# A ninth Strassen step in five gate units, E added by transfers, and last products by halves

## The chip, the cores and the metric

The kernel runs on one core of a Trainium2 chip. The metric is the device time of one execution in microseconds. Before the change three runs took 2383.65 to 2385.43 us, median 2385.24.

## The reference

One hybrid decoder block on 256 tokens with 4096 channels, all float32:

```
h    = rmsnorm(x, norm_w)
proj = h @ w_in                       # 4096 -> 20480: u_p z_p u_c b_c c_c z_c (2048 each), g_logit (8192)
y_pool = pool(u_p) @ pool_w * pool_scale * silu(z_p)      # causal means over 2, 4, 8, 16 tokens
y_conv = b_c * (conv_b + conv3(c_c * u_c)) * silu(z_c)
br     = [y_pool, y_conv] @ w_branch                      # two times 2048 -> 4096
merged = sum over n of sigmoid(g_logit[n] + gate_b[n]) * br[n]
x      = x + merged @ w_out                               # 4096 -> 4096
return rmsnorm(x, final_norm_w)
```

Nearly all of the work is in three matrix products, with w_in, w_branch and w_out.

## The kernel before, in words

**Units.** The work is cut into 32 units, each of which makes 1024 output columns for all 256 tokens (two halves of 128 tokens on the partitions) in the tile R. In order: the convolution's cu0 cc0 cz0 cb0 cu1 cc1 cz1 cb1, the pooling's pz0 pu0 pz1 pu1, the eight gate units g0_0 g1_0 g0_1 g1_1 g0_2 g1_2 g0_3 g1_3 (branch, then column block), eight branch units b0_0 to b1_3, and four output units o0 to o3. A unit with 4096 rows of weights has 16 steps of 256 rows. Each step loads 1 MB of weights into one of three raw buffers by SP's queue.

**P and S steps.** Float32 accuracy comes from splitting each operand into a high part, rounded to the fast matmul format (an ACT copy), and a low part (a DVE subtraction), and from three products, high by high, high by low, low by high. A plain step (P) multiplies 2 row blocks x 2 token halves x 2 column halves, 8 products of three matmuls of 128x512 each: 24 matmuls. A Strassen step (S) treats the same as a 2x2 block product with 7 products: 21 matmuls. It needs sums of weights and so more of DVE: an addition into V, two additions in raw, and subtractions 1536, 1024 and 1024 wide; a P step needs two subtractions 1024 wide. In the program's order on DVE an S step is: addition into V, addition in raw, the 1536-wide subtraction (from ACT's 1536-wide copy), addition in raw, subtraction from V, subtraction from raw.

**The ring.** The split weights lie in a ring of 60 blocks (256 columns each); an S step takes 28, a P step 16. `pump` hands out work for a step up to three steps ahead of PE, as far as the ring has room, and raw buffers are loaded again once their step is split. Every engine works through its own instructions in the written order (`keep_in_program_order`).

**x and its sums.** The split x stays in the arena: pairs of row blocks with sums for Strassen (S operands) and without (P operands). The arena has sums for 7 pairs. An eighth pair, `LATE` (number 8), has its sums made early by `late_sums`, put away in DRAM (`late_d`), and fetched and split again in g0_0 (`late_split`) into a pool that takes the place of the tile Y; from then on the gate units can have 8 S steps. In which steps a unit has S is set by `spread_sequence` or `at_places`: before, g0_1 to g0_3 had P S P S P S P S S P S P S P S P. Steps of a unit are numbered from 0.

**Ends of units, and ticks.** The banks `sums` (E banks) are emptied by ACT to the tile E with the factor rin; the four banks `shared`, which hold the other Strassen products, are joined into R by an ACT copy and four DVE additions and subtractions (`joins`). When the last step of a unit is P, the shared banks are closed a step earlier, and the joins are put on `queue` then ("early"). `queue` holds small pieces of work; one is taken after every 6 matmuls (a tick), and `gap(n)` leaves n ticks free. `combine` then adds E to R: for most gate units by two DVE additions, for g0_0 and o0 by a transfer that accumulates (`move_add`, POOL's queue), which needs no DVE. The gate's bias gate_b is always added by such a transfer. After that the unit's epilogue is queued: one free tick, the sigmoid of R on ACT, and a store of R to `gates_d` by POOL. All this runs beside the next unit's matmuls.

**The end.** The last three steps of o3 are done token half by token half. `finish_half` adds a bank to R and squares it on ACT with a sum over the columns; `finish` makes 1/rms from these sums, scales the four column blocks (three of them fetched back from DRAM) and stores them.

Of the kernel before, what the change touches and what calls it, by code (L numbers as in the profile page):

```python
# [32 lines left out]
P = 128  # L33
# [23 lines left out]
def hybrid_block(ctx: ExitStack, tc: tile.TileContext, x, x_t, norm_t, w_first, w_in, pool_w, pool_scale,  # L57
# [68 lines left out]

    y_d = dram.tile([2, 2, P, 4, 2, T], F32, name="y_d")
    m_d = dram.tile([4, P, 4, 2, T], F32, name="m_d")
    late_d = dram.tile([P, 5, P], F32, name="late_d")
    z_d = dram.tile([2, P, 2, NU], F32, name="z_d")  # L130
    o_d = dram.tile([3, P, 2, NU], F32, name="o_d")

# [9 lines left out]
    def replace_by(name, place=upper):  # L142
        close(upper)
        close(place)
        place["stack"] = stack = ExitStack()
        ctx.enter_context(stack)
        return stack.enter_context(tc.tile_pool(name=name, bufs=1))

    Y = replace_by("y", lower).tile([P, 2, NU], F32, name="Y")

# [319 lines left out]
    def combine(u):  # L470

        d = u.dst
        if u.s:
            early = u.flags.get("joined")
            if not early:
                join(u)
            if u.name.startswith(('cu1', 'cz', 'pz')):

                queue.append(lambda: move_add(d, E))
                queue.extend(gap(9))  # L480
            elif u.name in ['g0_0', 'o0']:
# [48 lines left out]
    def gap(n):  # L530
        return [None] * n
# [567 lines left out]

    LATE = NP_X - 1  # L1100

    def late_sums():
        o = x_ops[LATE]
        h, l = (o.view[:, part].bitcast(F32) for part in range(2))
        q = sa[:, 4:8].rearrange("p (k t) c -> p k t c", t=2)
        add(q, h, l)
        q = q.rearrange("p k t c -> p k (t c)")
        mul(q, q, rbc[:, None].to_broadcast([P, 2, T]))
        sums_s(sa, [sa[:, i] for i in range(4, 8)])
        mul(sa[:, Q3], sa[:, Q3], std)  # L1110
        move(late_d[:, 0:4], sa[:, 0:4])
        move(late_d[:, 4], sa[:, A11])
# [211 lines left out]
    for u in units:  # L1324
        if u.name == "pu1":
            make_bands(1)
        if u is last_x:
            Y = replace_by("y_b", lower).tile([P, 2, NU], F32, name="Y")
            stages.append(replace_by("more").tile([P, 4, P], F32, name="sb"))

            in_y = [Y.rearrange("p a n -> p (a n)")[:, i * 4 * P:(i + 1) * 4 * P].rearrange("p (k c) -> p k c", k=4) for i in range(2)]
            stages.extend(in_y)
        if u is last:
            break
        for st in u.steps:
            assert st.prepared, (u.name, st.kind)
            run_step(u, st)
            state["now"] += 1
            if u is last_x and st is u.steps[12]:
                units_done[0] = True  # L1340
            if u.s and not u.flags.get("joined") and st is not u.steps[-1] and u.closed(*SHARED):
                assert not queue, u.name
                queue.extend(joins(u))
            pump()
            if u is units[units.index(last_x) - 1] and st is u.steps[14]:
                queue_fills()
            if u.name == "g0_0" and st is u.steps[2]:
                move(sa[:, 0:5], late_d)
# [57 lines left out]
    for c in range(3):  # L1406
        unpark(c)

    pre, pre_h, var_h, dev = (sb(name, [P, 2]) for name in ("pre", "pre_h", "var_h", "dev"))

    def ts(dst, a, s1, s2, op0, op1=ALU.bypass):
        pin(nc.vector.tensor_scalar(out=dst, in0=a, scalar1=s1, scalar2=s2, op0=op0, op1=op1))

    def finish_half(t, n):

        w = NH // (1 + n)
        for i in range(1 + n):
            cs = slice(n * NH + i * w, n * NH + (i + 1) * w)
            add(R[:, t, cs], bank_of(("E", t, n))[:, i * w:(i + 1) * w], R[:, t, cs])
            act(V[:, n, i * w:(i + 1) * w], R[:, t, cs], AF.Square, accum_out=ossq[:, t, 3 + n + i:4 + n + i])  # L1420
        if n == 0:
            mul(E[:, t, 0:NH], R[:, t, 0:NH], Y[:, 0, 0:NH])

    def finish(t):
        q, h, r, s, v = (a[:, t:t + 1] for a in (pre, pre_h, rout, dev, var_h))
        part = ossq[:, t, 5:6]
# [10 lines left out]
        for c, queue_ in ((0, nc.sync), (1, nc.scalar), (2, nc.sync), (3, nc.sync)):  # L1437
            if c == 1:
                act(parked[c][:, t], parked[c][:, t], scale=r)
            elif c == 0:  # L1440

                for n in range(2):
                    v = parked[c][:, t, n * NH:(n + 1) * NH]
                    pin(nc.vector.tensor_scalar(out=v, in0=v, scalar1=r, scalar2=None, op0=ALU.mult))
                    pin(queue_.dma_start(of[t * P:(t + 1) * P, n * NH:(n + 1) * NH], v))
                continue
            elif c == 2:
                pin(nc.vector.tensor_scalar(out=parked[c][:, t], in0=parked[c][:, t], scalar1=r, scalar2=None, op0=ALU.mult))
            else:
                pin(nc.vector.tensor_scalar(out=E[:, t, 0:NH], in0=E[:, t, 0:NH], scalar1=r, scalar2=None, op0=ALU.mult))  # L1450
                stt(E[:, t, NH:NU], R[:, t, NH:NU], r, Y[:, 0, NH:NU], ALU.mult, ALU.mult)
            pin(queue_.dma_start(of[t * P:(t + 1) * P, c * NU:(c + 1) * NU], E[:, t] if c == 3 else parked[c][:, t]))

    for t in range(2):
        for ns in ((0, 1),) if t == 0 else ((0,), (1,)):
            for st in tail:
                st.toks, st.halves, st.final = (t,), ns, (t, ns[-1]) == (1, 1)
                while not st.op.ready:
                    pop_fill(True)
                for g in st.groups():  # L1460
                    multiply(last, st, g)
            for n in ns:
                finish_half(t, n)
        finish(t)


# [47 lines left out]
```

## Time and profile before

| what | value |
|---|---|
| median of three runs | 2385.24 us |
| the profiled execution | 2384.67 us, its span 2383.0 us |
| PE | 2370.5 us busy, 99% of the span, 10558 matmuls |
| DVE | 2136.1 us busy, 90% |
| ACT | 1380.5 us busy, 58% |
| POOL | 78.3 us busy, 3% |
| TensorE clock granted | 0.998 |
| DMA | 550.92 MB, mean 231 GB/s |

PE is the engine of the matmuls, DVE the vector engine, ACT the scalar engine, POOL and SP issue transfers. The busy time of PE is modelled: matmuls are pipelined and overlap, so the distance from one matmul's start to the next says more than the 390 ns that the profile gives to each. In a timeline row stand the start, the time taken, engine, line, operation, result and sources, shapes, how many were merged (x3), and in brackets how long the engine was idle before and for whom. Rows are merged when equal operations follow each other. In a row of the windows view stand the window, its length, and for each engine the busy time and the number of instructions, then the granted clock, the DMA share and GB/s. L72 is the helper of all DVE additions, subtractions and products, L69 that of ACT, L1244 that of the matmuls, L94 that of the accumulating transfers, L91 that of the others from POOL.

### The profile page before, as it was taken

How to read it: one execution, taken by the hardware profiler on the slowest of the kernel's cores; microseconds unless marked ns; L12 is line 12 of the kernel's file. 1: busy time of each engine (PE TensorE's matmuls, PEld its weight loads, DVE VectorE, ACT ScalarE, POOL GpSimd, SP SyncE). 2: the span in 40 equal slices, each digit the busy share in tenths (PEclk: the TensorE clock that was granted, in tenths of full speed). 3: DMA queues.
4: the chain of work that ended last, by engine and by line, in shares of the span. 5: the costliest groups of instructions: out<-in, count | busy, mean ns of one | idle time of the engine just before them, and what ended most of it. 6: DMA issues, size and time to landing. Idle time of an engine off the chain costs nothing.

```text
span 2383.0 us, 27859 instructions
## 1 busy us (share of the span) xinstructions
PE 2370.5 (99%) x10558; PEld 1961.5 (82%) x10558; DVE 2136.1 (90%) x2162; ACT 1380.5 (58%) x1443; POOL 78.3 (3%) x148
## 2 busy tenths in 40 slices
PE   9999999999999999999999999999999999999998
PEld 7888888888888888888888888888888888888886
DVE  8899989889989978979999999999898898798998
ACT  7555655556555556556565655566664556565564
POOL 0010000000000000000000000000100001000000
PEclk9999999999999999999999999999999999999999
DMA  8455665655666655755776677667766667567667
GB/s 336 170 207 195 233 243 199 225 202 211 230 228 214 233 192 212 242 191 201 256 248 219 232 236 238 226 239 259 264 250 229 227 251 285 210 215 253 244 241 262
DMA packets 83158, 550.92 MB, mean 231 GB/s; under 512 B 9536, under 2 KB 9536, under 8 KB 21584
## 3 DMA queue, kind: packets, MB, share of 16 engines
q1 hardware_dynamic: 68800, 484.51, 54.4%
q0 software_dynamic: 13792, 63.58, 9.6%
q8 instruction: 82, 1.34, 0.2%
q10 hardware_dynamic: 432, 1.07, 0.1%
q14 instruction: 52, 0.43, 0.1%
HBM read 516.28 MB, written 25.49 MB: 227 GB/s over the span
## 4 chain that ended last, share of the span: by engine, by line
PE 94%; issue 3%; DVE 1%; DMA 1%; ACT 0%; DVEq 0%; ACTq 0%; POOLq 0%
PE sums L1244 73%; PE shared L1244 19%; PE shared L746 1%; PE shared L509 1%; DVE ring L72 1%; DMA R<-in_x_dram 1%; DMA raw<-in_w_out_dram 0%; DMA R<-E 0%; ACT ring L69 0%; DVE V L72 0%; PE shared L1008 0%; DVE raw L72 0%; DVE R L72 0%; PE shared L725 0%; PE shared L726 0%
## 5 line engine op out<-in xcount | busy, mean ns | idle before, releaser
L1244 PE MATMUL sums<-ring,arena 128*128 128x512 f32 x8031 | 1888.2, 390 | 0.0
L1244 PEld LDWEIGHTS sums<-ring,arena 128*128 128x128 f32 x8031 | 1504.9, 188 | 313.2 <-ACT E L69 0.6
L69 ACT ACTIVATE ring<-raw 128x1024 fp32r<-128x1024 f32 (+2 forms) x902 | 994.9, 1142 | 729.9 <-DVE raw L72 290.0
L72 DVE TENSOR_TENSOR ring<-raw,ring 128x1024 fp32r<-128x1024 f32 (+2 forms) x902 | 1171.9, 1329 | 167.5 <-ACT ring L69 129.9
L1244 PE MATMUL shared<-ring,arena 128*128 128x512 f32 x2079 | 526.0, 389 | 0.5 <-DVE ring L72 0.5
L1244 PEld LDWEIGHTS shared<-ring,arena 128*128 128x128 f32 x2079 | 390.0, 188 | 82.1 <-DVE ring L72 1.3
L69 ACT ACTIVATE ring<-V 128x1024 fp32r<-128x1024 f32 x180 | 190.2, 1056 | 124.8 <-DVE V L72 91.1
L72 DVE TENSOR_TENSOR V<-raw 128x1024 f32<-128x1024 f32 x180 | 219.2, 1218 | 4.9 <-DMA raw<-in_w_in_dram 3.1
L72 DVE TENSOR_TENSOR ring<-V,ring 128x1024 fp32r<-128x1024 f32 x180 | 219.2, 1218 | 2.5 <-ACT ring L69 2.5
L72 DVE TENSOR_TENSOR raw<-raw 128x512 f32<-128x512 f32 x180 | 124.5, 692 | 6.2
L72 DVE TENSOR_TENSOR raw<-V,raw 128x512 f32<-128x512 f32 x180 | 124.3, 691 | 5.4
L72 DVE TENSOR_TENSOR R<-R,E 128x1024 f32<-128x1024 f32 (+1 forms) x49 | 77.6, 1590 | 1.6 <-ACT E L69 0.9
L72 DVE TENSOR_TENSOR R<-R,shared 128x512 f32<-128x512 f32 x87 | 59.5, 683 | 13.3 <-ACT R L69 9.5
L69 ACT ACTIVATE E<-sums,rin 128x512 f32<-128x512 f32 x76 | 50.7, 687 | 26.7 <-PE sums L1244 26.7
L69 ACT ACTIVATE arena<-sa 128x512 fp32r<-128x512 f32 (+2 forms) x42 | 22.4, 560 | 36.0 <-DVE sa L72 35.3
L72 DVE TENSOR_TENSOR arena<-sa,arena 128x512 fp32r<-128x512 f32 (+2 forms) x42 | 24.4, 604 | 1.4 <-ACT arena L69 1.4
L69 ACT ACTIVATE E<-sums 128x512 f32<-128x512 f32 x40 | 22.3, 593 | 4.8 <-PE sums L1244 4.4
L509 PEld LDWEIGHTS shared<-ident,R 128*128 128x128 f32 x160 | 19.4, 140 | 4.2
L509 PE MATMUL shared<-ident,R 128*128 128x128 f32 x160 | 22.6, 272 | 0.0
L746 PE MATMUL shared<-ring 128*128 128x512 f32 x96 | 22.1, 389 | 0.0
L69 ACT ACTIVATE R<-R 128x2048 f32<-128x2048 f32 x8 | 15.4, 1920 | 11.4 <-DVE R L72 7.6
L72 DVE TENSOR_TENSOR R<-R,Y 128x1024 f32<-128x1024 f32 (+1 forms) x16 | 21.5, 1355 | 0.3
(142 smaller groups left out, 467.8 us busy)
## 6 DMA issues: line engine op xcount, KB each, us to landing
raw<-in_w_in_dram SPq DMA_DIRECT2D x318, 1024.0 KB, 4.9
raw<-in_w_branch_dram SPq DMA_DIRECT2D x64, 1024.0 KB, 5.5
raw<-in_w_out_dram SPq DMA_DIRECT2D x64, 1024.0 KB, 5.0
R<-in_gate_b_dram POOLq DMA_DIRECT2D x8, 1024.0 KB, 11.7
gates_d<-R POOLq DMA_DIRECT2D x8, 1024.0 KB, 9.1
R<-E POOLq DMA_DIRECT2D x6, 1024.0 KB, 8.6
raw<-in_pool_w_dram SPq DMA_DIRECT2D x4, 1024.0 KB, 4.7
Y<-gates_d POOLq DMA_DIRECT2D x4, 1024.0 KB, 7.4
```

The lines of the kernel that those rows point to most:

```text
L69: return pin(nc.scalar.activation(dst, src, func, **kw))
L72: return pin(nc.vector.tensor_tensor(out=dst, in0=a, in1=b, op=op))
L509: pin(nc.tensor.transpose(shared(j)[:, i * T + t * P:i * T + (t + 1) * P], src[:, t, c:c + P], ident))
L746: pin(nc.tensor.matmul(o, a[:, k, ts], b[:, k], start=(k, i) == (0, 0), stop=(k, i) == (3, 2)))
L1244: pin(nc.tensor.matmul(ps, lhs, rhs, start=n == 0, stop=n == u.total[b] - 1))
```

## The change

Five gate units, g0_1, g1_1, g0_2, g1_2 and g0_3, get nine S steps of 16, in the order P P S S P S S P S S P S S P S P. For the ninth, pair 7's sums are made by a second call of `late_sums`, ahead of step 42 (cz0's step 10), and stored in a second DRAM tile; they are fetched and split in g1_0 (`second_split`), three blocks in the pool that stands in Y's place and two in a pool above it. The matrices for the pooling's windows (`make_bands`) are therefore made ahead of step 118 (cb1's step 6) instead of step 33, since they take the place of tiles that `late_sums` needs. `combine` adds E by the accumulating transfer for g1_0, g0_1, g1_1, g0_2 and g1_2 as well; where the joins were early, the transfer of gate_b is issued first, then that of E, and 12 ticks are left free instead of 17. At the end, the last step's products of the last bank are done 256 columns at a time, the second half in another bank, the mean for the square root gets a tile of its own and is made first, and the first output block is stored in 256 and 768 columns instead of 512 and 512.

```diff
-    late_d = dram.tile([P, 5, P], F32, name="late_d")
+    late_d = [dram.tile([P, 5, P], F32, name=f"late_d{i}") for i in range(2)]
...
-            elif u.name in ['g0_0', 'o0']:
+            elif u.name in ['o0', 'g0_0', 'g1_0', 'g0_1', 'g1_1', 'g0_2', 'g1_2']:
 
                 queue.append(lambda: move_add(d, E))
                 if not early:
                     queue.append(lambda: move_add(d, u.added))
-                queue.extend(gap(17))
+                queue.extend(gap(12 if early else 17))
...
         if (n, c) in ((0,1),(1,1),(0,2),(1,2),(0,3),(1,0),):
             seq = spread_sequence(NS_X + 1, 1 if c else 2)
+        if (n, c) in ((0,1),(1,1),(0,2),(1,2),(0,3),):
+            seq = at_places({2,3,5,6,8,9,11,12,14})
...
-    def late_sums():
-        o = x_ops[LATE]
+    def late_sums(i):
+        o = x_ops[LATE - i]
...
+    def second_place():
+        o = x_ops[LATE - 1]
+        o.more, tiles = {}, []
+        for pool, blocks in ((lower["pool"], (Q3, Q5, Q6)), (replace_by("late_too"), (Q7, A11))):
+            q = pool.tile([P, 2, len(blocks), P], F32R, name="more_sums")
+            tiles.append(q)
+            for i, b in enumerate(blocks):
+                o.more[b] = q[:, :, i]
+        return tiles
+
+    def second_split():
+
+        o, src, q = x_ops[LATE - 1], (sa[:, 0:3], sa[:, 3:5]), []
+
+        def high():
+            q.extend(second_place())
+            for a, b in zip(q, src):
+                act(a[:, 0], b)
+
+        def low():
+            for a, b in zip(q, src):
+                sub(a[:, 1], b, a[:, 0].bitcast(F32))
+            o.more_ready = True
+        return [high, low]
...
-    before(23, late_sums)
-    before(33, make_bands, 0)
+    before(23, late_sums, 0)
+    before(42, late_sums, 1)
+    before(118, make_bands, 0)
...
+            if u.name == "g1_0" and st is u.steps[4]:
+                move(sa[:, 0:5], late_d[1])
+            if u.name == "g1_0" and st is u.steps[7]:
+                queue.extend(second_split())
...
     def finish(t):
...
         pin(nc.vector.tensor_reduce(out=q, in_=ossq[:, t:t + 1, 0:5], axis=mybir.AxisListType.X, op=ALU.add))
+        ts(m, q, 1.0 / D, EPS, ALU.mult, ALU.add)
         ts(h, q, -0.5 / D, -0.5 * EPS, ALU.mult, ALU.add)
-        ts(q, q, 1.0 / D, EPS, ALU.mult, ALU.add)
-        act(s, part, AF.Sqrt, scale=1.0 / D, bias=q)
+        act(s, part, AF.Sqrt, scale=1.0 / D, bias=m)
...
-                for n in range(2):
-                    v = parked[c][:, t, n * NH:(n + 1) * NH]
+                for a, b in ((0, NH // 2), (NH // 2, NU)):
+                    v = parked[c][:, t, a:b]
...
+                if (t, ns) == (1, (1,)) and st is tail[-1]:
+
+                    (b, mm, _), = st.groups()
+                    for i in range(2):
+                        cs = slice(i * NH // 2, (i + 1) * NH // 2)
+                        for k, (lhs, rhs) in enumerate(mm):
+                            pin(nc.tensor.matmul(shared(0)[:, 0:NH // 2] if i else bank_of(b)[:, cs], lhs, rhs[:, cs],
+                                                 start=i == 1 and k == 0, stop=k == len(mm) - 1))
+                        if i == 0:
+                            add(R[:, t, NH:NU], bank_of(b), R[:, t, NH:NU])
+                        else:
+                            add(R[:, t, NH + NH // 2:NU], shared(0)[:, 0:NH // 2], R[:, t, NH + NH // 2:NU])
+                        finish_part(t, 1, i, False)
+                    continue
```

More of the change, by code (lines that the diff above doesn't have):

```diff
@@ L146, in replace_by @@
         ctx.enter_context(stack)
-        return stack.enter_context(tc.tile_pool(name=name, bufs=1))
+        place["pool"] = stack.enter_context(tc.tile_pool(name=name, bufs=1))
+        return place["pool"]
     Y = replace_by("y", lower).tile([P, 2, NU], F32, name="Y")
@@ L1110, in late_sums @@
         mul(sa[:, Q3], sa[:, Q3], std)
-        move(late_d[:, 0:4], sa[:, 0:4])
-        move(late_d[:, 4], sa[:, A11])
+        move(late_d[i][:, 0:4], sa[:, 0:4])
+        move(late_d[i][:, 4], sa[:, A11])
     def late_place(pool, o, blocks):
@@ L1347, in hybrid_block @@
             if u.name == "g0_0" and st is u.steps[2]:
-                move(sa[:, 0:5], late_d)
+                move(sa[:, 0:5], late_d[0])
             if u.name == "g0_0" and st is u.steps[8]:
@@ L1407, in hybrid_block @@
         unpark(c)
-    pre, pre_h, var_h, dev = (sb(name, [P, 2]) for name in ("pre", "pre_h", "var_h", "dev"))
+    pre, pre_h, var_h, dev, mean = (sb(name, [P, 2]) for name in ("pre", "pre_h", "var_h", "dev", "mean_out"))
     def ts(dst, a, s1, s2, op0, op1=ALU.bypass):
@@ L1414, in finish_half, with finish_part @@
     def finish_half(t, n):
-        w = NH // (1 + n)
         for i in range(1 + n):
-            cs = slice(n * NH + i * w, n * NH + (i + 1) * w)
-            add(R[:, t, cs], bank_of(("E", t, n))[:, i * w:(i + 1) * w], R[:, t, cs])
-            act(V[:, n, i * w:(i + 1) * w], R[:, t, cs], AF.Square, accum_out=ossq[:, t, 3 + n + i:4 + n + i])
+            finish_part(t, n, i)
         if n == 0:
             mul(E[:, t, 0:NH], R[:, t, 0:NH], Y[:, 0, 0:NH])
+    def finish_part(t, n, i, sums=True):
+        w = NH // (1 + n)
+        if True:
+            cs = slice(n * NH + i * w, n * NH + (i + 1) * w)
+            if sums:
+                add(R[:, t, cs], bank_of(("E", t, n))[:, i * w:(i + 1) * w], R[:, t, cs])
+            act(V[:, n, i * w:(i + 1) * w], R[:, t, cs], AF.Square, accum_out=ossq[:, t, 3 + n + i:4 + n + i])
     def finish(t):
         q, h, r, s, v = (a[:, t:t + 1] for a in (pre, pre_h, rout, dev, var_h))
+        m = mean[:, t:t + 1]
         part = ossq[:, t, 5:6]
         pin(nc.vector.tensor_reduce(out=q, in_=ossq[:, t:t + 1, 0:5], axis=mybir.AxisListType.X, op=ALU.add))
+        ts(m, q, 1.0 / D, EPS, ALU.mult, ALU.add)
         ts(h, q, -0.5 / D, -0.5 * EPS, ALU.mult, ALU.add)
-        ts(q, q, 1.0 / D, EPS, ALU.mult, ALU.add)
-        act(s, part, AF.Sqrt, scale=1.0 / D, bias=q)
+        act(s, part, AF.Sqrt, scale=1.0 / D, bias=m)
         ts(v, part, -0.5 / D, h, ALU.mult, ALU.add)
@@ L1440, in finish @@
             elif c == 0:
-                for n in range(2):
-                    v = parked[c][:, t, n * NH:(n + 1) * NH]
+                for a, b in ((0, NH // 2), (NH // 2, NU)):
+                    v = parked[c][:, t, a:b]
                     pin(nc.vector.tensor_scalar(out=v, in0=v, scalar1=r, scalar2=None, op0=ALU.mult))
-                    pin(queue_.dma_start(of[t * P:(t + 1) * P, n * NH:(n + 1) * NH], v))
+                    pin(queue_.dma_start(of[t * P:(t + 1) * P, a:b], v))
                 continue
@@ L1462, in hybrid_block @@
             for n in ns:
-                finish_half(t, n)
+                if (t, n) != (1, 1):
+                    finish_half(t, n)
         finish(t)
```

## The prediction

> **What bounds the kernel now.** I read the page first (the chain that ended last), then PE's waits, then the five units that change, by windows.
>
> ```profile
> PE 94%; issue 3%; DVE 1%; DMA 1%; ACT 0%; DVEq 0%; ACTq 0%; POOLq 0%
> ```
> ```profile
> PE shared L1244 <- DVE ring L72: 0.5, 2, 0.3
> ```
> ```profile
> 1205.89:1614.63 408.74, 408.74 (x1801) 337.92 (x1801) 380.06 (x353) 243.93 (x234) 9.41 (x11) 1.00 0.67 232
> 1287.67:1369.42 81.75, 81.75 (x362) 67.59 (x361) 75.76 (x71) 48.51 (x48) 1.76 (x2) 1.00 0.68 232
> ```
>
> The chain is PE, and PE waits for DVE only twice, 0.5 us in all. The third fence is gate units g0_1 to g0_3 together, then g1_1 alone; its columns are length, then busy time of PE, PEld, DVE, ACT, POOL, then clock. The clock is full; PE needs all of a unit's 81.75 us and DVE 75.76 of them. DVE is the only engine near PE, so the question is whether it still keeps up with more Strassen steps. The pace of both is in these rows of g1_1 (PE, then DVE):
>
> ```profile
> 1313.65 0.84 PE L1244 MATMUL shared<-ring,arena 128*128 128x512 f32 x3
> ...
> 1323.85 0.84 PE L1244 MATMUL shared<-ring,arena 128*128 128x512 f32 x3
> ```
> ```profile
> 1313.76 1.22 DVE L72 TENSOR_TENSOR V<-raw 128x1024 f32<-128x1024 f32 x1
> 1315.01 0.69 DVE L72 TENSOR_TENSOR raw<-V,raw 128x512 f32<-128x512 f32 x1
> 1315.62 1.75 DVE L72 TENSOR_TENSOR ring<-raw,ring 128x1536 fp32r<-128x1536 f32 x1
> 1317.41 0.69 DVE L72 TENSOR_TENSOR raw<-raw 128x512 f32<-128x512 f32 x1
> ...
> 1319.29 1.23 DVE L72 TENSOR_TENSOR ring<-raw,ring 128x1024 fp32r<-128x1024 f32 x1
> 1320.43 1.22 DVE L72 TENSOR_TENSOR V<-raw 128x1024 f32<-128x1024 f32 x1
> ...
> 1329.39 1.22 DVE L72 TENSOR_TENSOR V<-raw 128x1024 f32<-128x1024 f32 x1
> ...
> 1371.61 0.68 DVE L72 TENSOR_TENSOR R<-R,shared 128x512 f32<-128x512 f32 x1
> 1372.21 1.22 DVE L72 TENSOR_TENSOR ring<-raw,ring 128x1024 fp32r<-128x1024 f32 x1
> ```
>
> PE starts an S and a P step (45 matmuls) 10.20 us apart: 0.2267 a matmul, S 4.76, P 5.44. On DVE an S step takes 1320.43 - 1313.76 = 6.67, and S with P 1329.39 - 1320.43 = 8.96, so P 2.29; a 1024-wide operation takes 1.14 (1320.43 - 1319.29), one of a join 0.60 (1372.21 - 1371.61). DVE thus loses 1.91 on PE in an S step behind an S, and gains 3.15 in a P step.
>
> **The change: PE's saving.** Five P steps become S: 15 matmuls x 0.2267 = 3.40 us. A unit has 357 matmuls, 80.9 us.
>
> **DVE's sum.** 9 x 6.67 + 7 x 2.29 + 4 x 0.60 = 78.5 (before: 8 + 8 steps, joins, and 2 x 1.14 for E; 76.3 by these paces, 75.76 busy). The order is P P SS P SS P SS P SS P S P. Each P SS costs DVE 15.63 and PE 14.96, 0.67 lost; four are 2.7, which the ring can hold: PE's P P P at a unit's edge gives it back. With no other idle time DVE would keep up. So the new transfers decide.
>
> **The wait that the new transfers make.** E's addition on DVE (2.3 us a unit) goes away; instead POOL adds gate_b to R, then E to R, and ACT's sigmoid reads R after both. Rows:
>
> ```profile
> 1133.94 0.90 POOL L94 DMA_DIRECT2D R<-E  x1 [69.08 <-DVE R L72]
> 1144.01 1.20 POOL L94 DMA_DIRECT2D R<-in_gate_b_dram x1 [9.17 <-DMA R<-E]
> ...
> 1372.85 1.18 POOL L94 DMA_DIRECT2D R<-in_gate_b_dram x1 [58.42 <-DVE R L72]
> ```
> ```profile
> R<-in_gate_b_dram POOLq DMA_DIRECT2D x8, 1024.0 KB, 11.7
> ...
> R<-E POOLq DMA_DIRECT2D x6, 1024.0 KB, 8.6
> ```
> ```profile
> R<-E POOLq DMA_DIRECT2D x1, 1024.0 KB, 9.8
> ```
> ```profile
> 1311.61 1.92 ACT L69 ACTIVATE R<-R 128x2048 f32<-128x2048 f32 x1 [1.53 <-DVE R L72]
> 1313.43 1.48 ACT L69 ACTIVATE ring<-raw 128x1536 fp32r<-128x1536 f32 x1
> ```
> ```profile
> 1155.94 1.92 ACT L69 ACTIVATE R<-R 128x2048 f32<-128x2048 f32 x1 [3.75 <-DMA R<-in_gate_b_dram]
> ```
> ```profile
> 1158.83 1.23 DVE L72 TENSOR_TENSOR ring<-V,ring 128x1024 fp32r<-128x1024 f32 x1 [2.51 <-ACT ring L69]
> ```
>
> Two additions to R run one after the other (POOL waited 9.17 for the first). In g1_0, where they already do, ACT sat 3.75 us at the sigmoid, and behind it DVE 2.51, since ACT's next work is the high part from which DVE subtracts.
>
> Count from the join's last DVE operation (start 1371.61): gate_b is issued 1.24 later (1372.85), lands after 11.7; hand-over 0.27 (g1_0: 1144.01 less the 9.8 that the R<-E of 1133.94 took to land); R<-E 8.6; then sigmoid 1.82 (1313.43 - 1311.61) and the S step's 1536-wide act 1.48, with some 0.05 between engines: 25.2 us until DVE can subtract in step 6. In the changed program's order, the sigmoid stands directly ahead of that act, and DVE has before it: the join's end 0.60, 1.14 of step 2, step 3 (6.67), step 4 (2.29), step 5 (6.67), and two operations of step 6 (1.86): 19.2. So DVE idles 6.0 us in each of the five units. The gap of 12 ticks (72 matmuls, 16 us) puts ACT at the sigmoid some 20 us after the unit's start, but R is whole at 4.4 + 21.8 = 26.2.
>
> The 4.4 comes from this:
>
> ```profile
> 1367.17 0.68 ACT L69 ACTIVATE E<-sums,rin 128x512 f32<-128x512 f32 x1
> ...
> 1368.22 1.27 ACT L69 ACTIVATE E<-sums,rin 128x512 f32<-128x512 f32 x2
> ```
>
> ACT empties the first bank of step 15, three groups (18 matmuls, 4.1 us) before the unit ends, and copies a shared one: 1.05 (1368.22 - 1367.17) and some latency, so DVE's first join operation starts at -2.8; then 0.60, four operations of step 2 (1.25 + 0.61 + 1.79 + 0.61), 1.20 and 1.14 come before the last one.
>
> Behind POOL's waiting R<-E only gates_d is queued, needed first by the branch units; behind ACT's sigmoid, everything that DVE subtracts from.
>
> **What reaches PE.** First unit: DVE ends that subtraction at 4.4 + 25.2 + 1.75 = 31.35; PE wants it at the second matmul of step 6, 3 x 5.44 + 3 x 4.76 + 0.23 = 30.83: a stall of 0.5. From there DVE has no reserve, and the two later S pairs cost 0.67 each: 1.8. This leaves DVE some 1.5 us ahead at the unit's end (now 9), the join's last operation comes about 1.5 later, and from the second unit DVE is the bound: 78.5 + 6.0 = 84.5. Sum: 82.8 + 4 x 84.5 = 420.8 against 408.74: **+12.1**, PE's 3.40 within it.
>
> Bounds: the eight landings of gate_b run from 11.2 to 12.2, those of R<-E from 8.0 (in pu1) to the 9.8 above.
>
> ```profile
> DMA to landing us min/median/max: 11.2/11.7/12.2
> ```
> ```profile
> R<-E POOLq DMA_DIRECT2D x1, 1024.0 KB, 8.0
> ```
>
> With 11.2 and 8.0 DVE idles 4.9: 81.8 + 4 x 83.4, +6.7. With 12.2 and 9.8 it idles 7.7: 84.6 + 4 x 86.2, +20.7. I take the medians, of 8 and 6 transfers. More S steps also ask for weights faster while these land, which speaks for the upper part.
>
> The Trainium skill, page "DMA: Bandwidth & Descriptors", section "Anatomy of one DMA — SWDGE (gpsimd) path", fits 2.0 us plus bytes over 436 GB/s, an estimate of 4.4 us for these 1 MB. By it R would be whole some 15 us after the unit's start, ahead of ACT, and the first rival below would hold; the landings above disagree.
>
> **Moved work.** The second late_sums is 2.7 us of DVE and the bands 5.0:
>
> ```profile
> 120.06 0.69 DVE L72 TENSOR_TENSOR sa<-arena 128x512 f32<-128x512 f32 x1
> ...
> 122.77 1.22 DVE L72 TENSOR_TENSOR V<-raw 128x1024 f32<-128x1024 f32 x1
> ...
> 172.66 0.28 DVE L706 TENSOR_REDUCE cnt<-sa 128x1 f32<-128x128 f32 x1
> ...
> 177.65 4.62 DVE L72 TENSOR_TENSOR ring<-raw,ring 128x1024 fp32r<-128x1024 f32 x4
> ```
> ```profile
> 223.41 3.50 DVE L72 TENSOR_TENSOR ring<-raw,ring 128x1024 fp32r<-128x1024 f32 x3
> ...
> 623.63 3.49 DVE L72 TENSOR_TENSOR ring<-raw,ring 128x1024 fp32r<-128x1024 f32 x3
> ```
> ```profile
> 230.74 3.56 PE L1244 MATMUL sums<-ring,arena 128*128 128x512 f32 x15
> ...
> 628.32 2.20 PE L1244 MATMUL shared<-ring,arena 128*128 128x512 f32 x9
> ```
>
> late_sums falls in cz0 before step 10, whose first half DVE has at 225.8 (second of the three at 223.41) and PE wants at 231.4 (three matmuls into 230.74): 5.6 ahead, so 0 (2.7 without that cover). The bands go to cb1's step 6: its last subtraction ends at 624.9, and PE uses it 6 matmuls after 628.32, at 629.7: 4.8 ahead, so 5.0 costs 0.2 (bounds 0 and 5.0). POOL's selections go with them, past a queue that is empty there. The second split is two acts and two subtractions of 384 and 256 columns in g1_0, about 0.8 us on DVE (640 columns, between 0.60 for 512 and 1.14 for 1024), in a unit where PE waits for nothing; POOL's fetch of late_d[1] stands behind gate_b, ahead of gates_d, which waits for the sigmoid anyway: 0 (0.8 uncovered).
>
> **The end.**
>
> ```profile
> 2373.78 0.29 ACT L69 ACTIVATE dev<-ossq,pre 128x1 f32<-128x1 f32 x1 [0.26 <-DVE pre L1412]
> ```
>
> Twelve half-width matmuls stream as many columns as six full ones. The first addition, now 512 wide, starts earlier, but takes longer by about as much as it starts earlier; with the mean made first, the square root saves the 0.26 that it waited for DVE's pre. I take -0.3 (0, were the halves to give nothing and the wait to stay, to -0.7, with one 256-wide addition off the path). Cutting the first output row 256 and 768 wide instead of 512 and 512 moves the same bytes ahead of the last transfer: 0.
>
> **The sum:** 12.1 + 0.2 - 0.3 = +12.0 on the profiled execution's 2384.67: 2396.7. That run is 0.6 under the median 2385.24; I say 2396.
>
> **Rivals.** 1. *No wait that counts.* Only the savings stay: -3.40 - 0.3 + 0.2, 2381. It holds while DVE idles less than its 80.9 - 78.5 = 2.4 of slack, so while the two transfers take under 16.7 together. For it: DVE's sum fits into PE's. Against it: the least rows sum to 19.2. Break-even is an idle of 3.2 (81.75 - 78.5), transfers of 17.5; between it and the forecast (2383 to 2390) gain and stalls nearly cancel. 2. *Contention.* Both landings at their greatest rows or beyond: +20.7 and more, 2405 upward. 3. *The ring hides ACT's wait*, with rival 1's time; it would take 6 us of lead at step 6, where the SS pairs leave 4 to 5. In o1 it did not:
>
> ```profile
> 2159.51 1.23 DVE L72 TENSOR_TENSOR ring<-raw,ring 128x1024 fp32r<-128x1024 f32 x1 [5.24 <-ACT ring L69]
> ```
> ```profile
> 2166.47 0.73 PE L1244 MATMUL shared<-ring,arena 128*128 128x512 f32 x2 [0.30 <-DVE ring L72]
> ```
>
> There ACT's square waits for the same pair of transfers; DVE's 5.24 us of idleness used the ring up and PE waited, even with S and P in turn.
>
> **Chances.** The forecast with its own range, 2390 to 2404: 0.62. Rivals 1 and 3: 0.20. Cancelling, 2383 to 2390: 0.10. Rival 2: 0.08. About 0.2% (4.8 us) is what a measurement of this kernel can tell from no change; rival 1's 4 us is inside it. Hence faster 0.03, same 0.28, slower 0.69 (a little of the forecast lies under 2390). The range takes in most of rival 1: 2381 to 2403.
>
> **What would show it.** Right: ACT's R<-R idle for DMA R<-E some 5 to 8 us in g0_1 to g0_3; behind it a 1536-wide DVE subtraction idle 5 to 7 for ACT; PE idle for DVE at step 6 and at the second of each later S pair; gate_b's issues 84 to 85 apart instead of 81.75. Wrong: these issues 81 apart, or the sigmoid not waiting.

## The result and the profile after

The changed kernel takes 2412.18 us (median of four runs, 2411.34 to 2413.06), the kernel before on the same chip 2384.55: a ratio of 1.0118, 95% interval 1.0105 to 1.0130. I had forecast slower, 2396 us, and no more than 2403; the loss is more than twice the forecast one. The span of the profiled execution is 2411.3 us (before: 2383.0).

The chain of the changed kernel, by engine:

```profile
PE 79%; DVE 8%; DMA 6%; issue 5%; ACT 2%; DVEq 0%; ACTq 0%; POOLq 0%
```

Waits from the start of g0_1 to the start of g1_3 (the five units with nine S steps): total, times, longest, in us.

```profile
DVE ring L72 <- ACT ring L69: 39.3, 9, 8.7
ACT R L69 <- DMA R<-E: 33.8, 5, 8.5
...
PE shared L1273 <- ACT ring L69: 9.2, 4, 3.7
...
PE shared L1273 <- DVE ring L72: 7.1, 9, 1.3
...
PE sums L1273 <- ACT E L69: 1.2, 2, 0.9
```

The five units by windows (length, busy time of PE, PEld, DVE, ACT, POOL, then the granted clock):

```profile
1206.17:1291.20 85.03, 82.34 (x358) 66.78 (x357) 75.09 (x70) 48.09 (x46) 2.70 (x3) 1.00 0.67 228
1291.20:1379.99 88.79, 83.53 (x358) 67.92 (x357) 77.33 (x73) 49.18 (x47) 2.66 (x3) 0.98 0.65 223
1379.99:1464.85 84.86, 82.46 (x358) 66.71 (x357) 77.27 (x73) 49.85 (x48) 2.66 (x3) 1.00 0.69 237
1464.85:1553.31 88.46, 84.15 (x358) 68.55 (x357) 78.01 (x75) 49.89 (x48) 2.66 (x3) 0.96 0.67 229
1553.31:1642.29 88.98, 83.38 (x358) 67.63 (x356) 80.36 (x76) 49.75 (x48) 3.22 (x4) 0.98 0.67 230
```

They take 436.12 us together, 27.4 more than the 408.74 before. DVE is busy 388.06 us of that and idle 48.1 (before 28.7). Ahead of g0_1 the kernel is 0.3 us late, g1_3 adds 1.6, and from o3's first matmul to the end it takes 92.8 us where it took 93.3. So the loss lies in these units.

One of them, g1_1, shows the mechanism (the transfers and the sigmoid work on g0_1's R, beside g1_1's matmuls). First POOL, then ACT, DVE and PE:

```profile
1299.74 1.20 POOL L94 DMA_DIRECT2D R<-in_gate_b_dram  x1 [62.44 <-DVE R L72]
1311.44 0.90 POOL L94 DMA_DIRECT2D R<-E  x1 [10.51 <-DMA R<-in_gate_b_dram]
```
```profile
1323.20 1.91 ACT L69 ACTIVATE R<-R 128x2048 f32<-128x2048 f32 x1 [8.50 <-DMA R<-E]
1325.02 1.47 ACT L69 ACTIVATE ring<-raw 128x1536 fp32r<-128x1536 f32 x1
```
```profile
1326.52 1.76 DVE L72 TENSOR_TENSOR ring<-raw,ring 128x1536 fp32r<-128x1536 f32 x1 [8.69 <-ACT ring L69]
```
```profile
1326.54 0.50 PE L1273 MATMUL shared<-ring,arena 128*128 128x512 f32 x1 [3.70 <-ACT ring L69]
1328.33 1.22 PE L1273 MATMUL shared<-ring,arena 128*128 128x512 f32 x2 [1.29 <-DVE ring L72]
```

The two additions to R run one behind the other. ACT stands 8.50 us at the sigmoid for the second, DVE stands 8.69 us for the high part that ACT makes behind the sigmoid, and then PE waits twice.

Most of the time goes to the same place in every unit. PE in a unit without any wait needs 81.21 us (shown below by the first experiment). Over this the five units take 3.82, 7.58, 3.65, 7.25 and 7.77, together 30.1. By the starts of PE's steps, 22.6 of it lie at step 6 (the waits above and slower matmuls behind them), 2.7 at steps 9 and 12 (0.66 to 0.69 each, in g0_1 and g0_2), and 4.7 at the units' edges.

### The profile page after: what moved, and what is told of

Read it like the earlier page. It is cut to its first block, busy times and chain, and to the rows that moved or that the text cites. A ratio compares the mean times of both kernels' runs of the same rounds, so it can differ in the third digit from the quotient of the medians.

```text
span 2411.3 us, 27897 instructions
## 1 busy us (share of the span) xinstructions
PE 2378.9 (99%) x10549; PEld 1963.5 (81%) x10549; DVE 2146.9 (89%) x2181; ACT 1386.3 (57%) x1450; POOL 84.3 (3%) x156
## 4 chain that ended last, share of the span: by engine, by line
PE 79%; DVE 8%; DMA 6%; issue 5%; ACT 2%; DVEq 0%; ACTq 0%; POOLq 0%
PE sums L1273 61%; PE shared L1273 16%; DVE ring L72 4%; DMA R<-E 3%; DMA R<-in_gate_b_dram 2%; ACT ring L69 1%; DVE V L72 1%; DVE raw L72 1%; DVE R L72 1%; PE shared L747 1%; PE shared L510 1%; DMA raw<-in_w_in_dram 1%; DMA R<-in_x_dram 1%; DMA raw<-in_w_out_dram 0%; PE shared L1011 0%
## 5 line engine op out<-in xcount | busy, mean ns | idle before, releaser
L1273 PEld LDWEIGHTS shared<-ring,arena 128*128 128x128 f32 x2079 | 390.5, 188 | 103.2 <-DVE ring L72 11.9
L69 ACT ACTIVATE ring<-V 128x1024 fp32r<-128x1024 f32 x185 | 195.7, 1058 | 165.9 <-DVE V L72 137.8
L72 DVE TENSOR_TENSOR ring<-V,ring 128x1024 fp32r<-128x1024 f32 x185 | 225.3, 1218 | 8.0 <-ACT ring L69 8.0
L72 DVE TENSOR_TENSOR V<-raw 128x1024 f32<-128x1024 f32 x185 | 225.3, 1218 | 5.5 <-DMA raw<-in_w_in_dram 5.1
L72 DVE TENSOR_TENSOR R<-R,shared 128x512 f32<-128x512 f32 x87 | 59.4, 683 | 11.7 <-ACT R L69 8.1
L72 DVE TENSOR_TENSOR R<-R,E 128x1024 f32<-128x1024 f32 (+1 forms) x39 | 65.4, 1686 | 1.6 <-ACT E L69 0.9
L69 ACT ACTIVATE R<-R 128x2048 f32<-128x2048 f32 x8 | 15.3, 1916 | 38.9 <-DMA R<-E 33.8
L69 ACT ACTIVATE E<-sums 128x512 f32<-128x512 f32 x40 | 22.7, 593 | 5.5 <-PE sums L1273 4.9
L94 POOL DMA_DIRECT2D R<-E x11 | 9.9, 896 | 446.1 <-issue 323.6
L94 POOL DMA_DIRECT2D R<-in_gate_b_dram x8 | 9.7, 1208 | 381.4 <-DVE R L72 358.8
L510 PE MATMUL shared<-ident,R 128*128 128x128 f32 x160 | 22.6, 272 | 0.0
## 6 DMA issues: line engine op xcount, KB each, us to landing
R<-in_gate_b_dram POOLq DMA_DIRECT2D x8, 1024.0 KB, 11.2
```

The source lines that it names most:

```text
L69: return pin(nc.scalar.activation(dst, src, func, **kw))
L72: return pin(nc.vector.tensor_tensor(out=dst, in0=a, in1=b, op=op))
L94: return pin(nc.gpsimd.dma_start(dst, src, accum_op=ALU.add))
L510: pin(nc.tensor.transpose(shared(j)[:, i * T + t * P:i * T + (t + 1) * P], src[:, t, c:c + P], ident))
L1273: pin(nc.tensor.matmul(ps, lhs, rhs, start=n == 0, stop=n == u.total[b] - 1))
```

## The experiments

Three theories stood at the start. A: ACT stands at the sigmoid until both transfers have landed, and DVE idles behind it. B: nine S steps in SS pairs are more than DVE can follow. C: the weights' transfers are too slow for nine S steps.

**1. The sigmoid later.**

```diff
-                queue.extend(gap(12 if early else 17))
+                queue.extend(gap(20 if early else 17))
```

> The changed kernel with 20 free ticks instead of 12 after an early join, nothing else. Theory A (ACT stands at the sigmoid until gate_b and E have both landed, and DVE idles behind it): the sigmoid now comes some 31 us after the unit's start, R is whole at 29 to 32, so ACT's wait falls from 33.8 us in all to under 5, and the time to 2381 to 2386. Theory B (nine S steps with pairs overload DVE by themselves): 2408 to 2414, as before the edit. Theory C (the weights' transfers are too slow for nine S steps): 2395 to 2412, with ACT still waiting for raw.

Measured: 2382.40 us, a ratio of 0.9992 (0.9983 to 1.0002). With more rounds, below, the gain comes out just clear of the interval. The five units by windows, and DVE's wait for ACT in them:

```profile
1205.91:1611.95 406.04, 406.04 (x1787) 335.12 (x1785) 390.45 (x364) 250.25 (x236) 13.88 (x16) 1.00 0.72 246
```
```profile
DVE ring L72 <- ACT ring L69: 6.5, 6, 1.5
```

PE waits for nothing; the units take 2.70 us less than before the change. DVE's idle time for ACT fell from 39.3 to 6.5, with one constant changed. B and C fall as sole causes: the S steps, their order and their weights are those of the changed kernel.

**2. E added by DVE.**

```diff
-            elif u.name in ['o0', 'g0_0', 'g1_0', 'g0_1', 'g1_1', 'g0_2', 'g1_2']:
+            elif u.name in ['o0', 'g0_0']:
```

> The changed kernel with E added by DVE again in g1_0, g0_1, g1_1, g0_2 and g1_2; nine S steps kept. Theory A: no second transfer to wait for; DVE's sum is 78.5 + 2.3 = 80.8 us against PE's 80.9, so the long waits go and small stalls may stay: 2381 to 2390. Theory B: DVE has 2.3 us a unit more to do: 2412 to 2425. Theory C: one transfer of 1 MB a unit less: 2390 to 2405.

Measured: 2395.41 us, ratio 1.0047 (1.0032 to 1.0062). A missed this one: without the second transfer there should have been no loss. B missed it too. It lies in the range that C gave, but experiment 1 had already shown that the same weights need not cost anything. In g1_2 (DVE, then ACT, then DVE):

```profile
1481.41 1.22 DVE L72 TENSOR_TENSOR R<-R,E 128x1024 f32<-128x1024 f32 x1
```
```profile
1482.67 1.92 ACT L69 ACTIVATE R<-R 128x2048 f32<-128x2048 f32 x1 [4.53 <-DVE R L72]
```
```profile
1485.99 1.76 DVE L72 TENSOR_TENSOR ring<-raw,ring 128x1536 fp32r<-128x1536 f32 x1 [2.75 <-ACT ring L69]
```

The same wait has another cause here. DVE adds E behind the S pair's work, ACT waits 4.53 us for it at the sigmoid, and DVE then 2.75 us for ACT. Whether that, or DVE's greater sum, is the loss, experiment 7 asks.

**3. Eight S steps, E by transfers, and 4. eight S steps, E by DVE** (what is left is the rest of the change: sums, bands, end).

```diff
-        if (n, c) in ((0,1),(1,1),(0,2),(1,2),(0,3),):
-            seq = at_places({2,3,5,6,8,9,11,12,14})
```

> The changed kernel with the five gate units back at eight S steps; E still added by transfers there. Theory A: the sigmoid still waits for both transfers, DVE idles some 6 to 9 us behind it, but has 74.0 us of work in a unit of 81.75: 2385 to 2392, with most of ACT's wait still there. Theory B and C: 2384 to 2385, since the S steps are gone.

> Only what is left of the change: pair 7's sums made, stored, fetched and split (and not used), the bands at step 118, the end by halves; eight S steps and E by DVE as in the kernel before. All theories: 0.2 us for the bands, -0.3 for the end: 2384.0 to 2385.0.

Measured: 2388.13 us, ratio 1.0017 (1.0007 to 1.0026), for the first, as A expected; 2384.57, ratio 1.0002 (0.9993 to 1.0011), for the second, as all did. The windows and waits of the first:

```profile
1207.03:1619.86 412.83, 410.70 (x1800) 337.50 (x1801) 367.72 (x342) 240.82 (x232) 13.90 (x16) 1.00 0.70 243
```
```profile
DVE ring L72 <- ACT ring L69: 37.7, 10, 8.0
```

DVE idles almost as long for ACT as after the change (37.7 against 39.3 us), and the units lose only 4.1. With eight S steps DVE has 20 us less to do and takes most of the wait from its slack. Put together:

| five units against before, us | no long wait at the sigmoid | ACT waits for both transfers |
|---|---|---|
| eight S steps | 0 (before the change) | +4.1 (experiment 3) |
| nine S steps | -2.7 (experiment 1) | +27.4 (the change) |

Neither part costs much alone; together they do. (In the row of eight S steps DVE also adds E on the left, and not on the right.) The rest of the change is worth nothing that can be measured.

**5. Lighter weights while the transfers run.** Why do the transfers land so late? Theory D: the weights' transfers beside them. Rival F: the second of two such transfers is slow in any case.

```diff
+    LIGHT = ['g0_1', 'g1_1', 'g0_2', 'g1_2', 'g0_3']
...
-            load(r.rearrange("p (k n) -> p k n", k=2), s.src)
+            q = r.rearrange("p (k n) -> p k n", k=2)
+            if s.unit.name in LIGHT and s in s.unit.steps[4:9]:
+                load(q[:, :, 0:NU // 4], s.src[:, :, 0:NU // 4])
+            else:
+                load(q, s.src)
```

> Steps 4 to 8 of the five units that the transfers of gate_b and E fall into load only a quarter of each weight row (256 of 1024 columns; the rest of the buffer keeps the values of an older step, so those steps compute with wrong weights). All other work stays. Theory D: E's accumulating transfer lands late because the weights' transfers run beside it; with a quarter of their bytes it lands 8.0 to 8.7 us after its issue, as in the units where it runs alone, instead of the 10.2 to 12.6 seen after the change; ACT's wait for it falls from 33.8 us in all to 15 to 22, and the time to 2388 to 2400. Rival F: it takes this long whenever it stands right behind the transfer of gate_b on POOL's queue, whatever else runs: landings as before, 2409 to 2413.

Measured: 2385.12 us, ratio 1.0003 (0.9994 to 1.0013), below what D expected. First the transfers of one R<-E each, from its issue to the end of its landing, in the view of the DMA queues: the kernel before (g1_0), the changed kernel (g1_1), and this one (g1_1). q1 carries the weights.

```profile
q1 hardware_dynamic: 188, 1.41, 34.5%
...
R<-E POOLq DMA_DIRECT2D x1, 1024.0 KB, 9.8
```
```profile
q1 hardware_dynamic: 359, 2.56, 50.6%
...
R<-E POOLq DMA_DIRECT2D x1, 1024.0 KB, 11.7
```
```profile
q1 hardware_dynamic: 252, 0.24, 9.4%
...
R<-E POOLq DMA_DIRECT2D x1, 1024.0 KB, 8.0
```

And the medians from g0_1's to g1_3's start and a little beyond, of the changed kernel and of this one, then this one's wait at the sigmoid and its five units:

```profile
R<-in_gate_b_dram POOLq DMA_DIRECT2D x6, 1024.0 KB, 11.2
R<-E POOLq DMA_DIRECT2D x5, 1024.0 KB, 10.9
```
```profile
R<-in_gate_b_dram POOLq DMA_DIRECT2D x6, 1024.0 KB, 9.5
...
R<-E POOLq DMA_DIRECT2D x5, 1024.0 KB, 7.9
```
```profile
ACT R L69 <- DMA R<-E: 6.1, 5, 2.7
```
```profile
1205.98:1614.48 408.50, 406.50 (x1786) 334.79 (x1785) 388.31 (x362) 248.27 (x234) 13.88 (x16) 1.00 0.60 196
```

With 0.24 MB of weights beside it (steps 4 to 8 load a quarter) instead of 2.56 MB, the same transfer of E behind the same transfer of gate_b lands in 8.0 us instead of 11.7. D holds and F falls. It is below D's numbers because gate_b lands sooner too. The traces also show where E's transfer loses its time: ahead of its first packet on POOL's queue. In the five units of the changed kernel that packet moves 3.3 to 4.9 us after the issue (in g1_1 the window 1311.44 to 1314.90 has no packet of that queue, q0), in the six landings before the change 1.4 to 1.5 us after it, and here 1.5 to 1.7. From the first packet to the landing the five take 6.4 to 8.2 us and the six 6.5 to 8.3; here it is 5.5 to 6.5. So after the change E's transfer starts late more than it runs slowly. What holds the first packet back while weights are in flight the traces don't show. From gate_b's issue to the sigmoid's start it is now 16.8 to 18.0 us, 17.3 in the mean, against 21.7 to 23.8, 23.0 in the mean, after the change. The units come out 0.24 us under before.

**6. Sixteen ticks.**

```diff
-                queue.extend(gap(12 if early else 17))
+                queue.extend(gap(16 if early else 17))
```

> Sixteen free ticks instead of twelve ahead of the sigmoid in the five units, half of what the run with twenty had. Theory A (ACT stands at the sigmoid until both transfers have landed): ACT comes there 4 ticks x 1.36 = 5.4 us later, its wait falls from 6.8 us a unit to some 1.4, so 2383 to 2389. Rival: the loss hangs on DVE having no reserve at all, so that what is left of the wait, and the late weights at the units' edges, still cost most of it: 2393 to 2403.

Measured: 2398.06 us, ratio 1.0057 (1.0042 to 1.0072), within what the rival expected. ACT in g0_1, of the changed kernel and of this one:

```profile
1228.11 1.06 ACT L69 ACTIVATE ring<-raw 128x1024 fp32r<-128x1024 f32 x1 [2.01 <-DVE raw L72]
1234.51 1.92 ACT L69 ACTIVATE R<-R 128x2048 f32<-128x2048 f32 x1 [5.34 <-DMA R<-E]
```
```profile
1228.90 1.49 ACT L69 ACTIVATE ring<-raw 128x1536 fp32r<-128x1536 f32 x1 [0.55 <-PE sums L1273]
1234.29 1.92 ACT L69 ACTIVATE R<-R 128x2048 f32<-128x2048 f32 x1 [3.90 <-DMA R<-E]
1236.11 1.04 ACT L69 ACTIVATE ring<-V 128x1024 fp32r<-128x1024 f32 x1
```

A's sum of 5.4 us for four ticks was wrong. Ticks are counted in matmuls in the written order, and four of them moved the sigmoid behind one more instruction of ACT, the 1536-wide copy. ACT came there 1.2 us later here (at 1230.39 instead of 1229.17), and its wait for R<-E is 21.2 us in all instead of 33.8. What was left still cost 11.2 us in the five units. By 12, 16 and 20 ticks they stand at +27.4, +11.2 and -2.7 against before: each tick is worth about 4 us between 12 and 16 and 3.5 between 16 and 20.

**7. E by DVE, with the sigmoid later.** As experiment 2, and

```diff
                 queue.extend(halves(lambda t: add(d[:, t], d[:, t], E[:, t])))
+                if u.name in ('g1_0', 'g0_1', 'g1_1', 'g0_2', 'g1_2', 'g0_3'):
+                    queue.extend(gap(6))
```

> Nine S steps, E added by DVE as in the second experiment, and six free ticks between E's additions and the sigmoid. Theory G: what that experiment lost, it lost because ACT stood 4.5 us at the sigmoid for DVE's additions to R, and DVE then 2.8 us for ACT; with the sigmoid 8 us later this is gone and the time is 2383 to 2388. Rival B2: DVE's own sum with E's additions (79.7 us busy a unit of the 80.7 that PE needs) leaves nothing for the idle time at a unit's edge, wherever the sigmoid stands: 2391 to 2396.

Measured: 2390.10 us, ratio 1.0025 (1.0015 to 1.0035), between both theories. Its five units, and DVE's wait for ACT:

```profile
1205.74:1619.16 413.42, 408.58 (x1786) 334.26 (x1785) 399.20 (x373) 246.45 (x234) 9.44 (x11) 1.00 0.66 230
```
```profile
DVE ring L72 <- ACT ring L69: 5.5, 5, 1.4
```

DVE's wait for ACT is as short as in experiment 1, and the time fell by 5.3 us; the rest of the loss stays. DVE is busy 79.84 us a unit of the 81.21 that PE needs (the expectation's 80.7 was too low), and the 1.4 left don't cover its idle time, 14.2 us over the five. PE waits 4.8 us there, and 3.8 of it at units' starts, as B2 has it. So both theories hold a part: with E on DVE nine S steps still come out 4.7 us over before in these units, and the sigmoid has to stand where R is whole (9.6 over where it didn't, in experiment 2).

**8. E's transfer first.**

```diff
+    SWAP = ['g1_0', 'g0_1', 'g1_1', 'g0_2', 'g1_2']
...
-        more = [] if u.added is None or not early else [lambda: move_add(u.dst, u.added)]
+        more = [] if u.added is None or not early or u.name in SWAP else [lambda: move_add(u.dst, u.added)]
...
-                if not early:
+                if not early or u.name in SWAP:
```

> In the five units E's transfer is issued ahead of gate_b's; the ticks stay as they are. Theory D: E's transfer then runs right behind the join, where fewer weights are in flight, and lands in some 8.5 us, gate_b's in some 12 behind it; R is whole 2 to 3 us sooner than the 23.6 us after the change, and the time is 2396 to 2405. Rival F: the second of the two is the slow one whichever it is, R is whole after the same 23 to 24 us, 2408 to 2414.

Measured: 2405.80 us, ratio 1.0090 (1.0075 to 1.0105), between the two ranges. (The 23.6 in the expectation was a rough reading of one unit; the mean over five is 23.0.) In g1_1:

```profile
1298.23 0.85 POOL L94 DMA_DIRECT2D R<-E  x1 [62.32 <-DVE R L72]
1308.47 1.20 POOL L94 DMA_DIRECT2D R<-in_gate_b_dram  x1 [9.39 <-DMA R<-E]
```
```profile
1321.96 1.91 ACT L69 ACTIVATE R<-R 128x2048 f32<-128x2048 f32 x1 [6.61 <-DMA R<-in_gate_b_dram]
```

The pair takes 22.7 us in the mean, 0.3 less than the other way round: D's 2 to 3 us did not come, and F's forecast for R is the nearer one. E now lands sooner (8.4 to 11.0 us) and gate_b later (11.1 to 13.9). That this is the weights' doing, and not the place in the pair, is shown by experiment 5 and not by this one. Most of the 6.4 us that it is faster than the change must then come from elsewhere. With gate_b's transfer moved behind E's in the queue the sigmoid stands one tick later, a fault of the experiment (in g1_1 it came behind the 1536-wide copy), and by experiment 6 a tick is worth about 4 us; no run tests this by itself.

**9 and 10. Twenty-four ticks, and twenty again, in five rounds.** The edit is that of experiment 1, with 24 and with 20.

> Twenty-four free ticks. If ACT's wait for the two transfers is the only thing that the ticks act on (theory A), nothing is left to gain beyond twenty: the same time as with twenty, within 1 us. If a later sigmoid collides with something, such as the next unit's joins into R or the store to gates_d, it is slower: 2384 to 2390.

> The kernel of the first experiment once more (twenty free ticks), with more rounds, since its gain is near what can be measured. Its five units came out 2.7 us shorter than before the change and the kernel before has its end at about the same distance: 2381 to 2383 us, a ratio of 0.9988 to 0.9996. If the first measurement was luck: 2384 or more.

Measured: 2381.52 us with 24 ticks, 2381.49 with 20, both a ratio of 0.9990 (0.9981 to 0.9999). Beyond twenty nothing is left to gain, as A says, and the twenty ticks came out as expected. Both are faster than the kernel before by about 2.4 us, and than the change by about 30.

## Why the prediction was wrong

The sign and the mechanism were right; the size was not. Two terms of the sum were too small: the landing of the new R<-E, and what DVE needs for a unit apart from the wait. By the steps of the prediction:

- **PE's saving, -3.40.** Measured with all waits gone: -2.70. The S steps 2 and 3 take 4.89 and 4.90 us instead of 4.76. Their operands are the late pairs, which lie outside the arena, and groups of three matmuls start 0.70 us apart there (1216.80 to 1217.50) instead of 0.68. Before the change one step of each unit was such a step already, at 4.89, so that the second one is the 0.7 us that are missing. That the place of the operands is the cause was not tested.

```profile
1216.80 0.86 PE L1273 MATMUL shared<-ring,more_sums 128*128 128x512 f32 x3
1217.50 0.86 PE L1273 MATMUL sums<-ring,more_sums 128*128 128x512 f32 x3
```

- **DVE's sum, 78.5 a unit. This is one of the two steps that failed.** Busy 77.6, but of DVE's 48.1 us of idleness in the five units only 33.3 lie in the long waits behind the sigmoid. The other 14.8 us, 3.0 a unit, are four waits of 1.5 us for ACT near the units' ends (6.0 together), 2.9 us for raw weights, and short gaps; only these are inside the paces that the prediction added up. Experiment 1 has the same 15.6 us (406.04 less 390.45) without any loss, so that they don't come from the sigmoid. DVE thus needs 80.6 us of the 81.21 that PE needs: its reserve was 0.6 us a unit, and I had counted 2.4. "With no other idle time DVE would keep up" put this at nothing. One of the waits near a unit's end, in the changed kernel and in experiment 1:

```profile
1377.80 2.36 DVE L72 TENSOR_TENSOR ring<-raw,ring 128x1024 fp32r<-128x1024 f32 x2 [1.59 <-ACT ring L69]
```
```profile
1443.56 2.36 DVE L72 TENSOR_TENSOR ring<-raw,ring 128x1024 fp32r<-128x1024 f32 x2 [1.42 <-ACT ring L69]
```

- **The wait that the new transfers make. This is the other step that failed.** I took 11.7 for gate_b, 0.27 and 8.6 for E, 20.6 in all. They took 23.0, nearly all of the difference in E's: 9.9 to 12.3, median 10.9, where I had 8.6. My six landings of R<-E stood right behind a join, early in a unit, where few weights flow: 1.41 MB beside the slowest of them. The new R<-E starts some 12 us behind gate_b's, 18 to 20 us into the unit, and in g1_1 2.56 MB flow beside it. Two transfers of the trace of before ran as the second of such a pair, gate_b's in g1_0 (11.9) and R<-in_x_dram in o1 (13.0). Both are of another form, so I had a price for the form and none for the place. I wrote that more S steps ask for weights faster and that this speaks for the upper part, and took the median all the same.
- **DVE's idle time, 6.0 a unit.** Behind the sigmoid it was 5.54, 8.69, 5.05, 7.13 and 6.89 us, 33.3 in all and 6.7 a unit. (The 39.3 of the view above also holds the four waits near the units' ends.) I counted 19.2 us of DVE's work beside 25.2 us of chain; the chain was 2.4 longer. In g0_2, where the wait is shortest, the sigmoid stands behind the 1536-wide copy.
- **The period, 82.8 and then 84.5.** Measured 85.03, 88.79, 84.86, 88.46, 88.98, 87.2 in the mean; the two terms as measured, 80.6 + 6.7, give 87.3. The units came out 15.3 us longer than the sum said (436.12, not 420.8). By the sum itself 6.7 instead of 6.0 in five units is 3.5 of it, and 80.6 instead of 78.5 in the four units that DVE was to bound is 8.4; the remaining 3.4 are not taken apart. So the smaller part is the transfers' and the larger part the reserve that DVE did not have. On PE the lack of reserve shows at the units' edges: ACT waits for raw weights and the copy that frees an E bank stands behind it, so that PE begins late (4.7 us in all; rows of ACT and PE at g1_3's start):

```profile
1636.16 1.49 ACT L69 ACTIVATE ring<-raw 128x1536 fp32r<-128x1536 f32 x1 [2.44 <-DMA raw<-in_w_in_dram]
...
1641.57 0.67 ACT L69 ACTIVATE E<-sums,rin 128x512 f32<-128x512 f32 x1
```
```profile
1642.29 7.19 PE L1273 MATMUL sums<-ring,arena 128*128 128x512 f32 x24 [2.71 <-ACT E L69]
```

  The clock also falls behind the longer waits (last section); what that adds is not shown. That g1_3 loses 1.6 was not in the sum either: its first 24 matmuls, the row above, take 7.03 us (to 1649.32) instead of 5.44, at the low clock behind that wait.
- **The second late_sums at 0, the bands at 0.2.** This fits: PE waits for nothing ahead of g0_1 in the changed kernel, which starts it 0.28 us later than before, and in experiment 1 0.02 later.
- **The end, -0.3.** 0.5 us gained, within the bounds; the kernels of the experiments show 0.5 gained to 0.4 lost, so this is near what one profile can tell.
- **Rival 1 (no wait that counts).** Its break-even, transfers of 17.5 us together, came out near: experiment 5 has 17.3, and its units come out 0.24 us under before. That is luck in part. DVE's waits behind the sigmoid were only 1.3 us a unit there, where I had put break-even at 3.2 (81.75 - 78.5); with 80.6 in place of 78.5 it lies at 1.15.
- **Rival 2 (contention)**, with my chance of 0.08, came nearest in time, with its +20.7 "and more". It was half right in the mechanism: E's landings lay beyond their greatest row of before, gate_b's did not, and the larger part of the miss was DVE's reserve.
- **Rival 3 (the ring hides it)** fell: PE waited at step 6 in all five units, in four of them for ACT.
- **What would show it.** ACT's waits came out at 5.3 to 8.5, DVE's behind them at 5.1 to 8.7, the 0.67 at the later S pairs in g0_1 and g0_2, as written, though not in the other three units; gate_b's issues 83.6 to 89.0 apart, not 84 to 85.

## What to carry to other kernels

A landing time belongs to a place: take it from a transfer that runs where the new one will run, with the same traffic beside it, not from the median of the same form elsewhere. When a change spends an engine's slack and adds a wait in front of the same engine, price the pair and not the parts; here -2.7 and +4.1 made +27.4. Slack is what an engine has left after its work and after the idle time that stays in any case; here busy time alone left DVE 3.6 us a unit, and 0.6 were there. An engine that stands at an instruction for a transfer can often be helped by moving that instruction in the written order. Here eight more ticks turned 27.6 us of loss into 2.4 us of gain, and the free ticks had been counted for one transfer when two had to land.

## What the runs showed of the hardware that I had not expected

The granted clock can fall to half behind a stall. In g0_3 PE waited at step 6, for ACT and then for DVE. Its rows, and the windows from the second wait on, 1 us each:

```profile
1586.06 0.49 PE L1273 MATMUL shared<-ring,arena 128*128 128x512 f32 x1 [1.59 <-ACT ring L69]
1587.85 1.22 PE L1273 MATMUL shared<-ring,arena 128*128 128x512 f32 x2 [1.30 <-DVE ring L72]
```

```profile
1587.00:1588.00 1.00, 0.15 (x1) 0.15 (x1) 0.96 (x2) 0.00 (x0) 0.00 (x0) 0.69 1.10 393
1588.00:1589.00 1.00, 1.00 (x3) 0.81 (x4) 1.00 (x2) 0.36 (x1) 0.00 (x0) 0.50 1.01 266
1589.00:1590.00 1.00, 1.00 (x4) 0.81 (x3) 0.93 (x2) 1.00 (x2) 0.00 (x0) 0.50 0.81 250
1590.00:1591.00 1.00, 1.00 (x4) 0.77 (x4) 1.00 (x2) 1.00 (x2) 0.00 (x0) 0.61 0.04 16
```

What is missing to full clock, 0.31 + 0.50 + 0.50 + 0.39, comes to 3.4 us at half clock, and 1.4 us of it fall where PE has work. Behind them the clock is full again. It fell in g1_1, g1_2 and g0_3, the three long units (0.96 to 0.98 over the unit), and stayed at 1.00 in g0_1 and g0_2, where the waits at step 6 were 1.9 us and less. Part of it comes back: while PE is slow DVE gets ahead, and in the three units steps 9 and 12 have no stall. How much of the difference of some 3.8 us between the units is the clock's, no run takes apart; DVE, on which PE's stalls there hang, waits in these units for ACT and for raw weights, and nowhere directly for PE. The length of the wait alone does not decide: ahead of g1_3 a wait of 2.56 us in experiment 7 left the clock at 1.00 (1615 to 1625 us), and one of 2.58 us in experiment 6 took it to 0.61 over the next 4.3 us.

The Trainium skill, page "TensorE: Matmul & The Clock Gate", section "Part 1: The HAM clock gate", says that the clock is either full or half, in windows of about 3.4 us, and that it falls after an idle window. The half clock and its length agree with the rows above. That a whole idle window is needed doesn't. The first window above lacks 0.31, which is 0.62 us at half, so the clock fell at about 1587.4; until then PE had been idle for 1.59 and some 0.8 us, with a matmul between them.

An accumulating transfer of 1 MB inside the chip is slow even with little beside it. The landings are 8.0 us with 0.24 MB of weights and 11.7 with 2.56 MB; the least of all is 7.0, in g0_3 of experiment 5, with 0.03 MB. The Trainium skill, page "DMA: Bandwidth & Descriptors", section "Anatomy of one DMA — SWDGE (gpsimd) path", would make it an estimated 4.4 us; no landing here comes near, and load beside it adds 3.7 that the fit has no term for.
